# Block positions added to the tokens ahead of their split, and two more pieces ahead of the dilated groups' combination

## The chip, the cores and the metric

One core of a Trainium2 chip runs the whole kernel. The metric is device time in microseconds (us), from the start of one execution to its end. Engines are named as in the profile: PE is TensorE's matrix products, PEld its weight loads, DVE is VectorE, ACT is ScalarE, POOL is GpSimd, SP is SyncE, which issues the loads and stores.

## What is computed

One layer on 1024 tokens of width 1024. The input is projected by one wide matrix into the queries, keys and values of two mixers and their gates. Mixer A is attention in three dilated groups (dilation 1, 4, 16), whose outputs are weighted by a softmax over the groups' log-sums. Mixer B is sparse attention with three branches (compressed, selected, windowed). Both are merged by sigmoid gates, multiplied by an output matrix, normalised, and sent through a mixture of 32 experts, two for each token.

The change lies in two places: the combination of the dilated groups, and the compressed branch of mixer B. In the latter, blocks of 32 tokens with stride 16 (63 blocks, two key-value heads of width 64) get a learned position added to each token and go through a two-layer net:

```python
blocks = jnp.concatenate([chunks[:, r:r + n_cmp] for r in range(ratio)], axis=2)
blocks = blocks + pos_emb[:, None, :]
flat = blocks.transpose(0, 1, 3, 2, 4).reshape(B_, n_cmp, G, CMP_LEN * E)
return jax.nn.gelu(flat @ w1) @ w2
```

This is done twice, for keys ("k") and values ("v").

## The kernel before, in words

**Products in three passes.** Nearly every product of 32-bit data is made of three: both operands are split into a high part (a cast to the reduced 32-bit format, on ACT) and a low part (a subtraction, on DVE or POOL), and high x high, high x low and low x high are summed in PSUM. `split` (L120 to L125) does it for pages of 128x1024; its lines in the profile are L123 (ACT) and L124 (DVE or POOL).

**The stream and its pieces.** The projection is a list of 44 jobs, each one 128-column block of the input matrix (`jobs`, L519 to L533). `stream` (L222 to L242) runs a job as two halves of 512 tokens, each half as 8 steps over the contraction with three products (L233 to L235); every second step it yields. So a piece is six products, and a job is eight pieces. `chunk(n)` (L244) runs n pieces and counts them in `clock`. In the first piece of a job the next job's weights are split and the weights after that are loaded (`wsplit`, `wload`); there are two pages each for raw, high and low weights. When a half is complete, the job's sink takes it out of PSUM. The rest of the kernel up to the experts is written as a sequence of own products with `chunk` calls between them: the pieces fill TensorE's time while other engines work. The order of TensorE's instructions is exactly that of the program (L208). The other engines and SP are ordered by a planner from estimated times and the order of the program, and each then runs its queue in that order.

**The combination** (L554 to L614). The row statistics of the three dilated groups are turned by TensorE (12 groups of transposes, one piece behind each, L564 to L581), DVE and ACT make the group weights RW (L584 to L596), then `chunk(CCH)` with CCH = 6 runs at L597. Four rounds follow (L600 to L609): for each of three groups a product with a selector matrix (L605) spreads the weights over a bank (two banks, tag "pt"), DVE multiplies the group's output by it (L606), and POOL adds groups 1 and 2 onto group 0 (L609); one piece runs in each round, behind the second product. Each pair of rounds ends in a store (L610).

**The compression.** At L697 the pieces up to job 24 are run: `done` is 192, and the call runs `done - clock` of them, nine before. Then come the router's and gates' weights (loads L706 to L711, DVE and ACT L712 to L718, their product with ones L720, and products with the input, L739 and L740, with one piece behind each second step). During these pieces job 24, the tokens for k, is finished in two halves; job 26 brings those for v. Their sink is `cmp_sink` (L452 to L473): ACT copies the bank to a page "cr" (L455), then for each head, parity and half block ACT casts a strided view to CH (L469) and DVE subtracts to get CL (L470), eight of each per half. `compress` (L630 to L694) is a generator that is stepped between pieces: it loads the positions (L632), the second matrix (L635) and four pages of the first matrix (L639), splits these, and for each of 16 slices runs three products (L656 to L658). The positions do not pass through the tokens: DVE sums the slices of the first matrix, each row weighted by its position (L653, L655), into `acc`, and a product with a matrix of ones (L660) adds `acc` to each block's sum. Behind it come the activation (L663 to L669), transposes (L673), and the second matrix (L680, L688). The raw pages of the first matrix, "cr", and several others share four pages of tag "t".

Of the kernel before, what the change touches and what calls it, by code (L numbers as in the profile page):

```python
# [9 lines left out]
FP = mybir.dt.float32  # L10
# [4 lines left out]
OP = mybir.AluOpType  # L15
# [16 lines left out]
MG0 = 8  # L32
MG1 = 5
DLEAD = 3
CCH = 6
NLAG = 2
LEADW = 1
QEND = (15, 11)
# [39 lines left out]
def tile_hybrid(ctx: ExitStack, tc: tile.TileContext, x, xT, w_t, w_gate, pos_k, w1_k, w2_k, pos_v, w1_v, w2_v,  # L78
                w_a, w_b, w_out, w_oT, ln1_g, ln1_b, w_r, b_r, w_gu, w_dn, ln2_g, ln2_b, out, dbg=None):
    nc = tc.nc  # L80
# [78 lines left out]
    ones_f = k_pool.tile([128, 128], FP, name="ones_f")  # L159
# [15 lines left out]
    for k in range(8):  # L175
        r = s_pool.tile([128, 1024], FP, name=f"xr{k}")
        nc.sync.dma_start(r, xT[k * 128:(k + 1) * 128, :])
        raws.append(r)
        if k < 2:
            w = wraw("wr")  # L180
            nc.sync.dma_start(w, w_t[6 * k])
            first.append(w)
    for k in range(8):
        a, b = split(raws[k], xpage, xpage, "x")
# [264 lines left out]
            nc.sync.dma_start(mg[j, :, half * 512:half * 512 + 512], t)  # L449
        return sink  # L450

    def cmp_sink(CH, CL):  # L452
        def f(half, bnk):
            ps = tpage("cr", FP, (128, 512))
            nc.scalar.copy(ps, bnk)  # L455
            for g in range(2):
                v = ps[64 * g:64 * g + 64].rearrange("p (c l r) -> p r l c", l=8, r=2)
                for par in range(2):
                    b = slice(64 * par, 64 * par + 64)
                    for r in range(2):  # L460
                        c0, c1 = 32 * half, 32 * half + 32
                        if r == 0:
                            c1 = min(c1, 63)
                        else:
                            c0 = max(c0, 1)
                        src = v[:, par, :, c0 - 32 * half:c1 - 32 * half]
                        d = slice(63 * g + c0 - r, 63 * g + c1 - r)
                        hi = CH[b, 8 * r:8 * r + 8, d]
                        nc.scalar.activation(hi, src, AF.Copy)  # L469
                        nc.vector.tensor_tensor(CL[b, 8 * r:8 * r + 8, d], v[:, par, :, c0 - 32 * half:c1 - 32 * half],  # L470
                                                CH[64 * par:64 * par + 64, 8 * r:8 * r + 8, d].bitcast(FP),
                                                op=OP.subtract)
        return f  # L473

    C = {}
    N = []
    for G in range(2):
        sc = [[1.0 / (8.0 * BSLOPE[4 * G + 2 * p + i]) for i in range(2)] for p in range(2)]
# [25 lines left out]
    def c_sink(w):  # L504
        def sink(half, ps):
            if half == 0:
                C[w] = [t_pool.tile([128, 16, 126], FR, name=n, tag=n, bufs=1) for n in ("CH", "CL")]
            cmp_sink(*C[w])(half, ps)
        return sink

    def nsa_jobs(d):
# [16 lines left out]
    k, v, q = nsa_jobs(N[0])  # L528
# [98 lines left out]
    nc.vector.memset(kch.bitcast(FP), 0.0)  # L627
    nc.vector.memset(kcl.bitcast(FP), 0.0)

    def compress(pos, w1, w2, which):  # L630
        P = t_pool.tile([128, 16], FP, name="posT")
        nc.sync.dma_start(P, pos)  # L632
        W2 = t_pool.tile([128, 2, 2, 64], FP, name="w2")
        for i in range(2):
            nc.sync.dma_start(W2[:, :, i, :], w2)  # L635
        acc = t_pool.tile([128, 256], FP, name="sm", bufs=3)
        def prep(i):
            raw = tpage("w1")
            nc.sync.dma_start(raw.rearrange("p (l f) -> p l f", l=4), w1[:, 4 * i:4 * i + 4, :])  # L639
            return (raw,) + split(raw, thpage, tlpage, "w1")  # L640
        pre = [prep(0)]
        yield
        CH, CL = C[which]
        hp = bank("sc")
        for i in range(4):
            if i < 3:
                pre.append(prep(i + 1))
            raw, wh, wl = pre[i]
            for q in range(4):
                l = 4 * i + q  # L650
                f = slice(q * 256, q * 256 + 256)
                if l == 0:
                    nc.vector.tensor_scalar(acc, raw[:, f], P[:, 0:1], None, op0=OP.mult)  # L653
                else:
                    nc.vector.scalar_tensor_tensor(acc, raw[:, f], P[:, l:l + 1], acc, op0=OP.mult, op1=OP.add)  # L655
                nc.tensor.matmul(hp[:126, 0:256], CH[:, l, :], wh[:, f], start=l == 0, stop=False)  # L656
                nc.tensor.matmul(hp[:126, 0:256], CH[:, l, :], wl[:, f], start=False, stop=False)
                nc.tensor.matmul(hp[:126, 0:256], CL[:, l, :], wh[:, f], start=False, stop=False)  # L658
            yield
        nc.tensor.matmul(hp[:126, 0:256], ones_f[:, 0:126], acc, start=False, stop=True)  # L660
        u0 = t_pool.tile([128, 256], FP, name="sm", bufs=3)
        t = t_pool.tile([128, 256], FP, name="sm", bufs=3)
        nc.vector.tensor_copy(u0[:126], hp[:126, 0:256])  # L663
        nc.vector.tensor_tensor(t[:126], u0[:126], u0[:126], op=OP.mult)
        nc.vector.tensor_scalar(t[:126], t[:126], 0.044715, 1.0, op0=OP.mult, op1=OP.add)
        nc.vector.tensor_tensor(t[:126], t[:126], u0[:126], op=OP.mult)
        nc.scalar.activation(t[:126], t[:126], AF.Tanh, scale=math.sqrt(2.0 / math.pi))
        nc.vector.tensor_scalar(u0[:126], u0[:126], 0.5, None, op0=OP.mult)
        nc.vector.scalar_tensor_tensor(u0[:126], t[:126], 1.0, u0[:126], op0=OP.add, op1=OP.mult)  # L669
        yield  # L670
        pt = bank("pt")
        for ft in range(2):
            nc.tensor.transpose(pt[:, ft * 128:ft * 128 + 126], u0[:126, ft * 128:ft * 128 + 128], ident[:126, :126])  # L673
        u = t_pool.tile([128, 2, 2, 63], FP, name="sm", bufs=3)
        nc.scalar.copy(u.rearrange("p f g c -> p f (g c)"), pt[:, 0:256].rearrange("p (f m) -> p f m", f=2)[:, :, 0:126])
        yield
        ps = bank("av")
        if which == "k":
            for ft in range(2):
                nc.tensor.matmul(ps[:, :126], W2[:, ft].rearrange("p a e -> p (a e)"),  # L680
                                 u[:, ft].rearrange("p g c -> p (g c)"), start=ft == 0, stop=ft == 1)
            pv = ps[:, :126].rearrange("p (g c) -> p g c", g=2)
            nc.scalar.copy(kch[:, :, 0:63], pv)
            nc.vector.tensor_tensor(kcl[:, :, 0:63], pv, kch[:, :, 0:63].bitcast(FP), op=OP.subtract)
        else:
            for g in range(2):
                for ft in range(2):
                    nc.tensor.matmul(ps[0:63, g * 64:g * 64 + 64], u[:, ft, g, :], W2[:, ft, 0, :],  # L688
                                     start=ft == 0, stop=ft == 1)
            for g in range(2):  # L690
                nc.vector.memset(vcmp[g].bitcast(FP), 0.0)
                nc.scalar.copy(vcmp[g][0:63, 0:64], ps[0:63, g * 64:g * 64 + 64])
                nc.vector.tensor_tensor(vcmp[g][0:63, 64:128], ps[0:63, g * 64:g * 64 + 64],
                                        vcmp[g][0:63, 0:64].bitcast(FP), op=OP.subtract)  # L694

    done = 8 * (1 + 3 * 5 + MG0)
    chunk(done - clock[0])  # L697
    ck = compress(pos_k, w1_k, w2_k, "k")
    cv = compress(pos_v, w1_v, w2_v, "v")

    wr = tpage("wr", FP, (128, 8, 36))
    wb = t_pool.tile([128, 2, 36], FP, name="wb")
# [16 lines left out]
    ps = bank("sc")  # L719
# [1288 lines left out]
```

## Time and profile before

| what | value |
|---|---|
| median of 3 runs | 1700.71 us (1695.23 to 1700.79) |
| the profiled execution | 1701.19 us, span 1699.0 us |
| mean granted TensorE clock | 0.98 |
| PE busy | 1585.3 us (93% of the span) |
| DVE busy | 1252.2 us (74%) |
| ACT busy | 1114.8 us (66%) |
| POOL busy | 455.0 us (27%) |

The span reaches from the first to the last instruction. Busy times are summed over the whole span; where the engines stand in one stretch, a table by stretches tells. A wait is the idle time of an engine ahead of an instruction, put down to the instruction of another engine that ended last before it.

### The profile page before, as it was taken

What the parts mean: (1) busy time and instruction counts of PE and PEld (TensorE: products, weight loads), DVE (VectorE), ACT (ScalarE), POOL (GpSimd) and SP (SyncE); (2) the same over time, 40 slices, a digit from 0 to 9 for tenths busy, and PEclk for the clock granted to TensorE, in tenths of its full rate; (3) what the DMA queues carried; (4) which work ended last, traced back from release to release, by engine and by line L of the source; (5) the groups of instructions that cost most, each with busy time, mean ns of one, the idle gap of its engine ahead of it and who ended that gap; (6) DMA issues with size and microseconds to landing.
All of it is one profiled execution on the core that took longest, in us unless ns stands there. A gap on an engine that the chain in (4) does not pass through costs nothing. (4 is left out here: it accounts for less than half of the span.)

```text
span 1699.0 us, 24721 instructions
## 1 busy us (share of the span) xinstructions
PE 1585.3 (93%) x8109; PEld 1303.9 (77%) x8109; DVE 1252.2 (74%) x2740; ACT 1114.8 (66%) x2050; POOL 455.0 (27%) x416
## 2 busy tenths in 40 slices
PE   7999999998899999999789996999999999999991
PEld 6888888777778987788678995777777777777771
DVE  5555554247867774588877787889888998999994
ACT  4566665515557786477943112778898888889882
POOL 1011113341122333232620152133311231322242
PEclk9999999999999999999999997999999999999996
DMA  7111112232321010001363767999999999999982
GB/s 270 41 38 38 38 38 69 75 102 87 127 75 48 30 52 23 31 18 36 98 217 140 299 239 251 333 348 337 371 353 367 333 351 359 360 348 357 370 260 61
DMA packets 107362, 313.86 MB, mean 185 GB/s; under 512 B 22028, under 2 KB 26252, under 8 KB 107232
## 3 DMA queue, kind: packets, MB, share of 16 engines
q1 hardware_dynamic: 93936, 287.21, 46.4%
q0 software_dynamic: 13296, 25.05, 6.0%
q8 instruction: 65, 1.06, 0.3%
q14 instruction: 65, 0.53, 0.1%
HBM read 290.02 MB, written 46.98 MB: 198 GB/s over the span
## 5 line engine op out<-in xcount | busy, mean ns | idle before, releaser
L1507 DVE TENSOR_TENSOR el<-er,eh 128x1024 fp32r<-128x1024 f32 x384 | 448.6, 1219 | 36.3 <-ACT eh L1506 36.1
L1506 ACT CAST eh<-er 128x1024 fp32r<-128x1024 f32 x384 | 391.3, 1055 | 46.3 <-PE pt L1524 34.1
L233 PE MATMUL pp<-xh,wh 128*128 128x512 f32 x672 | 273.4, 407 | 1.6 <-DVE q L288 1.6
L235 PE MATMUL pp<-xh,wl 128*128 128x512 f32 x672 | 265.6, 395 | 0.0
L234 PE MATMUL pp<-xl,wh 128*128 128x512 f32 x672 | 264.2, 393 | 0.0
L1524 PE MATMUL av<-eh,xt 128*128 128x512 f32 x512 | 196.5, 394 | 1.5 <-ACT xt L1493 1.3
L1524 PE MATMUL pt<-eh,xt 128*128 128x512 f32 x512 | 197.2, 395 | 0.0
L235 PEld LDWEIGHTS pp<-xh,wl 128*128 128x128 f32 x672 | 127.1, 189 | 29.5
L233 PEld LDWEIGHTS pp<-xh,wh 128*128 128x128 f32 x672 | 127.4, 190 | 21.1 <-DVE q L288 2.0
L234 PEld LDWEIGHTS pp<-xl,wh 128*128 128x128 f32 x672 | 127.5, 190 | 19.5
L1524 PE MATMUL sc<-eh,at 128*128 128x512 f32 x512 | 142.1, 399 | 0.0
L898 POOL TENSOR_TENSOR pw<-pw,st 128x64 f32<-128x64 f32 (+5 forms) x128 | 86.0, 701 | 183.5 <-DVE st L893 154.3
L1550 POOL DMA_INDIRECT ybuf<-y,idx x30 | 84.8, 2827 | 173.6 <-ACT y L1549 166.3
L1524 PEld LDWEIGHTS av<-eh,xt 128*128 128x128 f32 x512 | 96.5, 189 | 24.9 <-ACT xt L1493 1.7
L1524 PEld LDWEIGHTS pt<-eh,xt 128*128 128x128 f32 x512 | 96.6, 189 | 22.7
L936 DVE TENSOR_TENSOR PT<-pt,PT 128x512 fp32r<-128x512 f32 (+1 forms) x136 | 91.0, 671 | 25.1 <-ACT PT L935 23.5
L1524 PEld LDWEIGHTS sc<-eh,at 128*128 128x128 f32 x512 | 93.3, 188 | 20.7 <-ACT eh L1506 0.8
L1524 PE MATMUL av<-el,xt 128*128 128x512 f32 x256 | 106.3, 415 | 3.0 <-DVE el L1507 2.2
L1524 PE MATMUL pt<-el,xt 128*128 128x512 f32 x256 | 101.0, 394 | 0.0
L124 POOL TENSOR_TENSOR wl<-wr,wh 128x1024 fp32r<-128x1024 f32 x24 | 59.0, 2459 | 137.4 <-ACT wh L123 118.0
L1401 POOL DMA_INDIRECT xg<-hbuf,idx x31 | 32.7, 1054 | 216.4 <-PE pp L1487 204.2
L935 ACT CAST PT<-pt 128x512 fp32r<-128x512 f32 (+1 forms) x136 | 76.8, 567 | 16.5 <-PE pt L928 14.9
(451 smaller groups left out, 3611.4 us busy)
## 6 DMA issues: line engine op xcount, KB each, us to landing
er<-in_w_gu_dram SPq DMA_DIRECT2D x256, 512.0 KB
er<-in_w_dn_dram SPq DMA_DIRECT2D x128, 512.0 KB
wr<-in_w_t_dram SPq DMA_DIRECT2D x44, 512.0 KB
mgd<-mg SPq DMA_DIRECT2D x32, 256.0 KB
G<-mgd SPq DMA_DIRECT2D x32, 256.0 KB
xr<-in_xT_dram SPq DMA_DIRECT2D x8, 512.0 KB
out_dram<-in_ln_b_dram SPq DMA_DIRECT2D x8, 512.0 KB
wo<-in_w_oT_dram SPq DMA_DIRECT2D x8, 512.0 KB
```

The source lines that it names most:

```text
L124: (eng or nc.vector).tensor_tensor(lo, raw, hi.bitcast(FP), op=OP.subtract)
L233: nc.tensor.matmul(ps, wh[:, kk], xh[k][:, c], start=k == 0, stop=False)
L234: nc.tensor.matmul(ps, wh[:, kk], xl[k][:, c], start=False, stop=False)
L235: nc.tensor.matmul(ps, wl[:, kk], xh[k][:, c], start=False, stop=k == 7)
L898: nc.gpsimd.tensor_tensor(t, t, st[:, 1, hi_, i:i + 1].to_broadcast([128, w]), op=OP.mult)
L935: nc.scalar.copy(t[:, 0], src)
L936: nc.vector.tensor_tensor(t[:, 1], src, t[:, 0].bitcast(FP), op=OP.subtract)
L1401: nc.gpsimd.indirect_dma_start(out=t, out_offset=None, in_=hbuf, in_offset=bass.IndirectOffsetOnAxis(ap=ids, axis=0), bounds_check=S - 1, ...
L1506: nc.scalar.copy(wh, r)
L1507: nc.vector.tensor_tensor(wl, r, wh.bitcast(FP), op=OP.subtract)
L1524: nc.tensor.matmul(pss[h], a[j == 1][:, kk], (wl if j == 2 else wh)[:, h], start=o == 0 and j == 0, stop=o == n - 1 and j == 2)
L1550: s_ = nc.gpsimd.indirect_dma_start(out=ybuf, out_offset=bass.IndirectOffsetOnAxis(ap=self.ids, axis=0), in_=y, in_offset=None, bounds_che ...
```

## The change

Positions are added to the tokens in the sink, in place of the weighted sum. The bank is read by DVE twice, once with the positions of the first 16 tokens of a block (r = 0) and once with those of the last 16 (r = 1), into one page of twice the width; the casts and subtractions read the one that belongs to their half block. `acc`, its 32 instructions for both tables and the product with ones go. The position table is now held as 32 values for each of the 64 channels, once for each head, and loaded in the first half of the sink by four loads (head x parity), in place of one load in `compress`; the table has one buffer. CCH goes from 6 to 8, so that `chunk(done - clock[0])` behind the combination runs two pieces fewer.

```diff
-CCH = 6
+CCH = 8
...
-    def cmp_sink(CH, CL):
+    def cmp_sink(CH, CL, pos):
         def f(half, bnk):
-            ps = tpage("cr", FP, (128, 512))
-            nc.scalar.copy(ps, bnk)
+
+            ps = tpage("cr", FP, (128, 2, 512))
+            for r in range(2):
+                nc.vector.tensor_tensor(ps[:, r].rearrange("p (c o) -> p c o", o=16), bnk.rearrange("p (c o) -> p c o", o=16),
+                                        pos[:, 16 * r:16 * r + 16][:, None, :].to_broadcast([128, 32, 16]), op=OP.add)
             for g in range(2):
-                v = ps[64 * g:64 * g + 64].rearrange("p (c l r) -> p r l c", l=8, r=2)
+                vs = [ps[64 * g:64 * g + 64, r].rearrange("p (c l r) -> p r l c", l=8, r=2) for r in range(2)]
...
-                        src = v[:, par, :, c0 - 32 * half:c1 - 32 * half]
+                        src = vs[r][:, par, :, c0 - 32 * half:c1 - 32 * half]
...
                 C[w] = [t_pool.tile([128, 16, 126], FR, name=n, tag=n, bufs=1) for n in ("CH", "CL")]
-            cmp_sink(*C[w])(half, ps)
+                P[w] = t_pool.tile([128, 32], FP, name="posT")
+                for g in range(2):
+                    o = P[w][64 * g:64 * g + 64].rearrange("p (l r) -> p l r", r=2)
+                    for par in range(2):
+                        nc.sync.dma_start(o[:, :, par], dict(k=pos_k, v=pos_v)[w][64 * par:64 * par + 64, :])
+            cmp_sink(*C[w], P[w])(half, ps)
...
-    def compress(pos, w1, w2, which):
-        P = t_pool.tile([128, 16], FP, name="posT")
-        nc.sync.dma_start(P, pos)
+    def compress(w1, w2, which):
...
-        acc = t_pool.tile([128, 256], FP, name="sm", bufs=3)
...
-                if l == 0:
-                    nc.vector.tensor_scalar(acc, raw[:, f], P[:, 0:1], None, op0=OP.mult)
-                else:
-                    nc.vector.scalar_tensor_tensor(acc, raw[:, f], P[:, l:l + 1], acc, op0=OP.mult, op1=OP.add)
...
-                nc.tensor.matmul(hp[:126, 0:256], CL[:, l, :], wh[:, f], start=False, stop=False)
+                nc.tensor.matmul(hp[:126, 0:256], CL[:, l, :], wh[:, f], start=False, stop=l == 15)
...
-        nc.tensor.matmul(hp[:126, 0:256], ones_f[:, 0:126], acc, start=False, stop=True)
```

## Rows read from the trace of the kernel before

**Rows 1.** Busy time by stretch: stretch, length, engines (instructions), PEclk, DMA share, GB/s

```profile
345.00:361.00 16.00, 12.72 (x40) 8.42 (x39) 10.90 (x17) 2.43 (x4) 8.08 (x8) 0.79 0.31 91
...
400.00:428.00 28.00, 22.17 (x113) 18.49 (x114) 22.96 (x38) 13.18 (x24) 5.37 (x6) 0.94 0.24 76
428.00:466.00 38.00, 33.18 (x170) 27.41 (x169) 34.30 (x54) 19.50 (x31) 7.13 (x4) 0.96 0.41 134
...
500.00:600.00 100.00, 99.86 (x640) 89.01 (x639) 75.84 (x251) 76.20 (x168) 36.35 (x36) 1.00 0.11 39
...
1200.00:1300.00 100.00, 98.16 (x443) 75.70 (x441) 88.55 (x109) 88.75 (x120) 23.12 (x14) 1.00 0.99 361
```

**Rows 2.** PE's waits, 300 to 500 us: us in total, times, longest

```profile
PE sc L660 <- DVE sm L655: 6.0, 2, 3.0
PE sc L657 <- DVE w1l L124: 2.9, 3, 1.9
PE pt L605 <- DVE rw L596: 1.9, 1, 1.9
PE sc L658 <- DVE CL L470: 1.6, 1, 1.6
```

**Rows 3.** Timeline of PE at the combination: start us, us, what, [idle before]

```profile
347.67 1.07 PE L605 MATMUL pt<-rw,sel 100*128 100x512 f32 x2 [1.87 <-DVE rw L596]
...
361.22 0.40 PE L233 MATMUL pp<-xh,wh 128*128 128x512 f32 x1
...
373.49 0.34 PE L720 MATMUL sc<-wb,ones_f 128*128 128x72 f32 x2
```

**Rows 4.** PE by the microsecond: stretch, length, busy, PEclk, DMA share, GB/s

```profile
349.00:350.00 1.00, 1.00 (x5) 0.73 0.00 0
...
356.00:357.00 1.00, 0.65 (x3) 0.86 0.00 0
```

**Rows 5.** Timeline of DVE behind the combination's products

```profile
358.50 1.98 DVE L606 TENSOR_TENSOR oT<-pt,oT 128x512 f32<-128x512 f32 x3 [0.93 <-PE pt L605]
...
369.61 0.69 DVE L715 TENSOR_TENSOR wgd<-wg,wgd 128x512 fp32r<-128x512 f32 x1 [3.91 <-ACT wgd L714]
```

**Rows 6.** Timeline of POOL at the combination's end

```profile
362.80 1.31 POOL L609 TENSOR_TENSOR oT<-oT,oT 128x512 f32<-128x512 f32 x1
...
364.93 2.43 POOL L124 TENSOR_TENSOR wl<-wr,wh 128x1024 fp32r<-128x1024 f32 x1
```

**Rows 7.** Timeline of SP's queue, same stretch: time of issue, queue time

```profile
358.65 0.74 SPq L708 DMA_DIRECT2D gbc<-in_ln_g_dram  x1
...
365.00 0.79 SPq L711 DMA_DIRECT2D wg<-in_w_gate_dram  x1
...
367.78 0.42 SPq L632 DMA_DIRECT2D posT<-in_pos_k_dram  x1
```

**Rows 8.** Timeline of PE at the end of the first compression

```profile
413.24 0.39 PE L233 MATMUL pp<-xh,wh 128*128 128x512 f32 x1
...
417.82 1.22 PE L660 MATMUL sc<-sm,ones_f 128*126 128x256 f32 x2 [3.03 <-DVE sm L655]
418.47 0.99 PE L233 MATMUL pp<-xh,wh 128*128 128x512 f32 x1
...
421.28 0.39 PE L233 MATMUL pp<-xh,wh 128*128 128x512 f32 x1
```

**Rows 9.** Two lines' instructions (ns min/median/max), and DVE's timeline at the activation chain's end

```profile
L655 DVE SCALAR_TENSOR_TENSOR sm<-w,posT,sm x30: 466/484/2703, 402.3 to 455.0; 128x256 f32<-128x256 f32 x30
...
L470 DVE TENSOR_TENSOR CL<-cr,CH x32: 567/586/1516, 385.0 to 440.2; 64x256 fp32r<-64x256 f32 x16, 64x248 fp32r<-64x248 f32 x16
...
422.24 0.42 DVE L669 SCALAR_TENSOR_TENSOR sm<-sm 126x256 f32<-126x256 f32 x1 [0.16 <-ACT sm L667]
```

**Rows 10.** Timeline of SP's queue ahead of the experts

```profile
932.82 8.94 SPq L1251 DMA_DIRECT2D z<-in_x_dram  x3
941.80 4.09 SPq L1559 DMA_DIRECT2D er<-in_w_gu_dram  x7
```

More of the change, by code (lines that the diff above doesn't have):

```diff
@@ L469, in f @@
                         nc.scalar.activation(hi, src, AF.Copy)
-                        nc.vector.tensor_tensor(CL[b, 8 * r:8 * r + 8, d], v[:, par, :, c0 - 32 * half:c1 - 32 * half],
+                        nc.vector.tensor_tensor(CL[b, 8 * r:8 * r + 8, d], src,
                                                 CH[64 * par:64 * par + 64, 8 * r:8 * r + 8, d].bitcast(FP),
@@ L473, in cmp_sink @@
         return f
-    C = {}
+    C, P = {}, {}
     N = []
@@ L697, in tile_hybrid @@
     chunk(done - clock[0])
-    ck = compress(pos_k, w1_k, w2_k, "k")
-    cv = compress(pos_v, w1_v, w2_v, "v")
+    ck = compress(w1_k, w2_k, "k")
+    cv = compress(w1_v, w2_v, "v")
     wr = tpage("wr", FP, (128, 8, 36))
```

## The prediction

> **What bounds the kernel now.** I read the stage table first [rows 1]. Between 500 and 600 us TensorE is busy 99.86 of 100 us: before the experts, the order of TensorE's work, written out by hand, is the clock of the kernel. From 1200 us on TensorE is busy 98.16 of 100 us at 361 GB/s; nothing in that part has a fixed date, its loads follow buffers that earlier work frees. So a microsecond that TensorE saves before 500 us should arrive at the end nearly whole. The three stretches that the diff touches stand out as holes: 345 to 361 us (12.72 of 16 busy, mean clock 0.79), 400 to 428 (22.17 of 28) and 428 to 466 (33.18 of 38). In the last two VectorE is busy 22.96 of 28 and 34.30 of 38 us: there it is the fullest engine. The list of TensorE's waits between 300 and 500 us names what ends the holes [rows 2]: 6.0 us in two waits of the ones product (L660) for the weight sums, 2.9 in three for the low part of a weight page (L657 on L124), 1.9 in one for the combination's first selector product (L605), 1.6 in one for the low part of the compressed tokens (L658). That is 12.4 us of bare waiting.
>
> The clock adds to it. Behind the 1.87 us wait before L605 [rows 3] the granted clock falls from 1.0 to half (1.2 GHz) between 349.5 and about 356.5 us [rows 4]. Behind the first L660 wait six ordinary products take 2.81 us, from 418.47 to 421.28 [rows 8], where full rate needs 6 x 0.227 = 1.36: 1.45 us lost.
>
> **Two more pieces (CCH).** A piece is six products; nine of them fill 361.22 to 373.49 us, 1.363 us each [rows 3]. Two more ahead of the combination are 2.73 us of work in front of L605, more than the 1.87 us wait. The weights RW it waits for do not depend on pieces, so the wait goes: **+1.87**. The combination itself runs 347.67 to 361.22, 13.55 us, half of it at half clock. At full clock its own work on TensorE is 12 products of 0.23 and four pieces of 1.36, 8.2 us; VectorE's 12 multiplies at 0.66 us [rows 5] are 7.9. With two banks, three products and a piece cannot repeat faster than piece, product, multiply, product: about 2.8 us, four times, 10.6 to 11 in all with the hand-overs. I take **+2.7**, ends 0 (the clock falls anyway) and 4.
>
> The two pieces are taken from behind the combination, where they are cover: seven are left of nine. What they cover is the gate and router weight: its low part (L715) ends at 369.61 + 0.69 = 370.30 us [rows 5], TensorE needs it right behind L720 at 373.49 [rows 3]. 3.2 us of slack less 2.73 leaves 0.5. Three things now lean on that slack. The weight job whose end frees a page now ends inside the combination (piece 184, third of its four, instead of first behind it), so the 2.43 us split on POOL (L124, at 364.93) can come ahead of POOL's last additions (one stood at 362.80) [rows 6], and the clearing of wg and its load (L711, 365.00) stand behind those. The freed page lets the next 512 KB weight load go earlier, beside wg's. And the position loads: below. Each could make wg 1 to 3 us late. Nearest is the POOL term, one split less the half that fits in gaps: I take a wait of **-1.5**, ends 0 and -5 (2.4 + 3.0 - 0.5). Sum of this part: 1.87 + 2.7 - 1.5 = **+3.1**.
>
> **Positions on the tokens.** Removed from VectorE: 30 multiply-adds at 0.484 us median [rows 9] and two first multiplies, for which I take no more than a multiply-add each: about 15 us. Removed from ACT: four copies of 128x512 (L455). Added to VectorE: eight additions of 128x512, one input in PSUM. Nearest is L606 at 0.66 (same shape, same memories): 5.3 us. The upper end is L470's rate, 0.586 for 256 strided columns, 1.17 each, 9.4 in all; I take 5.3, since both inputs run through 16 neighbouring elements before a jump. Either way VectorE is relieved, by 6 to 10 us. In the path through the sink ACT's copy of that shape becomes an addition of 0.66 ahead of ACT's first cast and a second that runs beside it; ACT in return has a copy less to do there. I count the sink as even.
>
> Then, on TensorE: both L660 waits go, **+6.0**; L660's own two passes take 417.82 to 418.47 = 0.65, twice [rows 8], **+1.3**; the half-clock stretch behind each, 1.45, twice, **+2.9** (the second taken like the first). The L657 waits come from VectorE doing sums ahead of a split: of 2.9 us I leave 1.2 (the splits still stand behind the token subtractions, and the second page of v behind its load), **+1.7**. The L658 wait arose as subtractions queued behind sums: of 1.6 I leave 0.3, **+1.3**. Next late is the activation chain (L663 to L669) that the transposes need: it now starts when the last L658 ends, and has a piece from 413.24 us plus three more, 5.4 us, for 3.6 us of its own (from 419.04, the end of L660, to 422.24 + 0.42 [rows 8, 9]) and three nk subtractions in the queue; **-0.5** for both halves, ends 0 and -5. Sum: 6.0 + 1.3 + 2.9 + 1.7 + 1.3 - 0.5 = **+12.7**.
>
> Nothing is charged for the shorter life of the raw weight pages (they are free after their split, no longer after the sums): it can only bring loads forward.
>
> **The position loads.** One load of 8 KB each (0.42 us of SP's queue at 367.78) becomes four of 4 KB whose elements land 8 bytes apart. The row nearest to that is the load of ln gains, 1024 elements of 4 bytes: 0.74 us of SP's queue [rows 7]. So some 3 us of SP per table instead of 0.4. For k they have from about 367 to 383 us, for v from the second k sink to the first v sink, some 30 us. I charge nothing beyond the term in the 1.5 above; ahead of L711 they would cost up to 3.0. The Trainium skill speaks against this load: "DMA: Bandwidth & Descriptors", section "Rules for kernel authors", says that a last dimension that is not contiguous becomes one descriptor per element. The trace agrees so far that the ln load held the queue longer than the contiguous one (0.74 against 0.42). By the page the term would stand at its lower end and the sum would be 3.5 us smaller.
>
> **Sum.** 3.1 + 12.7 = 15.8 us. The profiled execution took 1701.19 us (span 1699.0 and 2.2 around it), 0.5 above the median of 1700.71. 1701.19 - 15.8 = 1685.4, or 1684.9 from the median: I say 1685. A measurement here tells about 0.5%, 8.5 us, from no change.
>
> **Rivals.**
> 1. *The gate weight becomes the new wait.* POOL's split and the position loads both come ahead of wg: 5 us of wait at L739, and the clock falls behind it as it did behind 1.87 us (some 7 us at half, 3.4 lost). The first part turns from +3.1 to -3.8, and the total is 8.9: 1692. For it: only 0.5 us of slack is left. Against: wr, the ln gains and wg come earlier in the program than the position loads. Chance 0.17.
> 2. *The activation chain takes the place of the sums.* The mask work and nk subtractions that filled VectorE between sums stand ahead of L663; each half waits 2.5 us and drops the clock. -5 and -2.9: total 8.4, 1692. For it: VectorE is 90% busy at 428 to 466. Against: 15 us of that go away. Chance 0.15.
> 3. *Slower, by a new order of the loads at the experts' start.* All queues but TensorE's are ordered by a planner's own estimates, which shift from here on. At 932.82 three row loads (z) stand just ahead of a run of seven expert loads (941.80) on SP [rows 10]. If the plan puts expert loads ahead of z, the row stage that makes the routing starts later by 512 KB at 361 GB/s, 1.45 us for each. Eleven, 16 us, give all of the gain back; from there on it is slower, and seventeen, 24.7 us, end at 1710. For it: SP alone is planned there. Against: the row loads come first in the program. Chance 0.06.
> 4. *More than the sum:* no wait at wg and none at page starts, +1.5 + 1.5 + 0.5, and the combination at its upper end, +1.3: 1680. Chance 0.12.
> 5. *The sums go but their waits stay*, as the subtractions of the token sinks, now behind two additions, hold the splits: L660's terms (10.2) and 3.1 remain, less 1.5: total 11.8, 1689. Chance 0.12.
>
> My forecast, within 4 us of 1685, has the remaining 0.38. Faster by over 0.5% means below 1692.2: the forecast, 4 and 5, and half of 1 and 2, with the spread of the runs (1695.23 to 1700.79) about even: 0.75. Slower is rival 3: 0.06. The rest, 0.19, is the same. The range from 1677 to 1697 takes in all rivals but the third, and the ends of the unknown terms (0 to 4, 0 to -5, 0 to -5) as far as they don't fall together.
>
> **What would show it.** Right: no wait before L605 and clock 1.0 through the combination; L660 and L655 gone; the activation chain starting within 0.5 us of the last L658; L739 waiting under 2 us; the eight additions near 0.66 us. Wrong: a wait of over 3 us at L739 or L720, waits of over 2 us at L673, half clock in either stretch, additions over 1 us, or a hole of this size that opens behind 500 us.

## The result, and the profile after

The changed kernel takes 1687.2 us (median of five runs, 1685.11 to 1688.29) where the kernel before takes 1700.64 (1694.92 to 1700.79): a ratio of 0.9936 [0.9921, 0.9951], 13.4 us less. The profiled execution took 1687.2 us, its span is 1685.3 instead of 1699.0. I had said 1685.0 us, from 1677 to 1697.

The diff moves line numbers. In the kernel after, the combination's product is L613 (L605 before), its multiply L614, POOL's additions L617; the token subtractions are L473 (L470), the new additions L457; the three products of the compression are L657, L658 (the one with a page's low part) and L659 (L656 to L658). From L661 on the numbers are those of before.

Busy time by stretch, kernel after (columns as in [rows 1]):

```profile
345.00:361.00 16.00, 14.33 (x61) 10.81 (x60) 11.80 (x18) 3.88 (x6) 10.24 (x9) 1.00 0.28 102
...
400.00:428.00 28.00, 28.00 (x141) 23.93 (x140) 19.32 (x30) 17.28 (x28) 9.04 (x9) 0.94 0.22 48
428.00:466.00 38.00, 36.23 (x190) 29.43 (x189) 29.39 (x40) 19.68 (x30) 4.91 (x2) 1.00 0.55 181
500.00:600.00 100.00, 99.86 (x659) 89.53 (x658) 76.98 (x246) 76.53 (x174) 33.06 (x35) 1.00 0.12 40
```

The holes of [rows 1] are nearly filled: TensorE works 14.33, 28.00 and 36.23 us where it worked 12.72, 22.17 and 33.18, and the clock of the first stretch went from 0.79 to 1.00. VectorE is no longer the fullest engine from 400 to 428 us (19.32, was 22.96). One figure did not move, the 0.94 of the clock from 400 to 428, but its place did: the half clock stood behind the first wait at L660 and now stands behind the wait for k's first page.

TensorE's waits from 300 to 500 us, kernel after (us in total, times, longest):

```profile
PE sc L658 <- DVE w1l L124: 2.2, 2, 2.0
PE pt L613 <- DVE oT L614: 1.7, 3, 0.6
PE av L769 <- DVE wol L758: 1.5, 2, 0.8
PE sc L739 <- DVE wgd L715: 1.1, 1, 1.1
PE sc L659 <- DVE CL L473: 0.8, 1, 0.8
```

Of [rows 2], the wait for RW (1.9) and both waits for the sums (6.0) are gone. L739 on wgd is new, as forecast (1.12 us). A 2.0 us wait for a page's low part stays. Where they stand, in TensorE's timeline (start us, us, what, [idle before]):

```profile
348.56 0.62 PE L613 MATMUL pt<-rw,sel 100*128 100x512 f32 x2
...
359.13 0.40 PE L613 MATMUL pt<-rw,sel 100*128 100x512 f32 x1
...
369.30 0.44 PE L720 MATMUL sc<-wb,ones_f 128*128 128x72 f32 x2 [0.22 <-DVE wb L718]
370.86 0.50 PE L739 MATMUL sc<-xh,wgd 128*128 128x512 f32 x1 [1.12 <-DVE wgd L715]
...
399.35 0.38 PE L658 MATMUL sc<-w1l,CH 128*126 128x256 f32 x1 [2.03 <-DVE w1l L124]
...
431.73 0.39 PE L659 MATMUL sc<-w1h,CL 128*126 128x256 f32 x1 [0.83 <-DVE CL L473]
```

**How the gain builds up.** TensorE's order is fixed, so I compare kernels by marks: the start of one instruction on TensorE, counted from the last transposes of the row statistics (L569 before, L577 after; at 335.6 to 337.5 us in all kernels, and nothing ahead of them changes). Us behind that point, worked out from TensorE's timelines:

| mark | before | after | gained up to here |
|---|---|---|---|
| first selector product | 12.03 | 12.71 | (two more pieces, 2.73, ahead of it) |
| last selector product | 25.34 | 23.28 | |
| first product with the gate weight, L739 | 37.99 | 35.01 | 2.98 |
| first page of k | 64.49 | 61.14 | 3.35 |
| activation's transposes, k | 88.38 | 80.32 | 8.06 |
| first page of v | 102.73 | 94.65 | 8.08 |
| activation's transposes, v | 126.48 | 112.42 | 14.06 |
| first product of the sparse attention | 153.78 | 140.69 | 13.09 |

From that last mark to the end of the span it takes 1209.6 us before and 1208.8 after: in these two profiles what was gained ahead of 490 us arrives whole, as read from [rows 1]. But over all the kernels below, this same unedited stretch takes 1203.0 to 1210.8 us in single profiles, in no order that follows the edits. So parts are judged by marks, and only whole kernels by their ratios.

### The profile page after: what moved, and what is told of

Read it like the earlier page. It is cut to its first block, busy times and chain, and to the rows that moved or that the text cites. A ratio compares the mean times of both kernels' runs of the same rounds, so it can differ in the third digit from the quotient of the medians.

```text
span 1685.3 us, 24695 instructions
## 1 busy us (share of the span) xinstructions
PE 1583.9 (94%) x8105; PEld 1305.3 (77%) x8105; DVE 1241.6 (74%) x2716; ACT 1113.4 (66%) x2046; POOL 469.6 (28%) x416
## 3 DMA queue, kind: packets, MB, share of 16 engines
q8 instruction: 65, 1.06, 0.3%
## 5 line engine op out<-in xcount | busy, mean ns | idle before, releaser
L1550 POOL DMA_INDIRECT ybuf<-y,idx x30 | 103.3, 3444 | 172.0 <-ACT y L1549 151.0
L124 POOL TENSOR_TENSOR wl<-wr,wh 128x1024 fp32r<-128x1024 f32 x24 | 57.6, 2402 | 135.0 <-ACT wh L123 129.2
```

The lines of the kernel that those rows point to most:

```text
L124: (eng or nc.vector).tensor_tensor(lo, raw, hi.bitcast(FP), op=OP.subtract)
L1550: s_ = nc.gpsimd.indirect_dma_start(out=ybuf, out_offset=bass.IndirectOffsetOnAxis(ap=self.ids, axis=0), in_=y, in_offset=None, bounds_che ...
```

## The experiments

Two theories stood at the start. Mine: the two parts of the change act each in its own stretch, sizes as in the sum. The rivals: the wait at L739 comes from the position loads rather than from the moved pieces, and the page wait that stays is a matter of loads or clock rather than of VectorE's queue.

**Two more pieces alone (cch_only).**

```diff
-CCH = 6
+CCH = 8
```

> The kernel before with CCH = 8 and nothing else. Theory: the two edits add up, and this one is worth the 2.8 us by which the products with the input (L739) come earlier in the changed kernel: no wait before the first selector product, clock 1.0 through the combination, and a wait of 0.5 to 1.5 us at L720 or L739 remains, because the weight split on POOL now stands ahead of POOL's last additions and the router weights' loads wait behind those. Ratio to before about 0.998. Rival: the new wait at L739 comes from the four position loads on SP's queue; then it is gone here and the gain is 4.2 us. Second rival: the two pieces are worth nothing alone, since the cover they take from behind comes due in full; then L739 starts within 0.5 us of where it started before.

Measured: 0.9979 [0.9964, 0.9993]. L739 stands at 34.71 against 37.99, 3.28 us earlier, and 3.11 of it are still there at v's transposes (123.37 against 126.48). TensorE's timeline of this kernel:

```profile
370.94 0.44 PE L720 MATMUL sc<-wb,ones_f 128*128 128x72 f32 x2 [0.18 <-DVE wb L718]
372.23 0.50 PE L739 MATMUL sc<-xh,wgd 128*128 128x512 f32 x1 [0.84 <-DVE wgd L715]
```

No position load is changed here, yet 0.84 of the 1.12 us of wait is there: the moved pieces make it.

**Positions alone (pos_only)**: the kernel after with `CCH = 6`.

> The changed kernel with CCH = 6. Theory: the 1.87 us wait before the selector product and the half clock behind it are back, L720 and L739 wait for nothing, and the first transposes of the second activation (L673, v) come 11 us earlier than before; ratio to before 0.993 to 0.995 by its own gain of 10 to 11 us. The 2 us wait at the first page of k and the half clock behind it stay, since they depend on the sink and not on the pieces. Rival: the gain of the positions needs the pieces (the state of the clock or the planner's order differs), and the ratio is above 0.997.

Measured: 0.9943 [0.9925, 0.9961]. 1.88 us of wait for RW are back, none at L739 (37.15). At v's transposes it is 13.71 us ahead of before (112.77), where I had expected 11. The parts alone give 3.11 and 13.71, together 16.8; the change gives 14.06, 2.8 less. Of that, 1.1 is missing already at L739, mostly because the combination took 12.48 us here and 13.31 before, behind the same wait: its half clock was shorter in this profile. Another 1.4 is missing between the first page of k and k's transposes: 17.67 us here, 19.18 after (and 0.15 that cch_only loses there). Both kernels wait 2.0 us for the first page there, but only the kernel after has half clock behind it; I had expected it in both. TensorE's clock by the microsecond (stretch, length, busy, PEclk, DMA share, GB/s), after and then pos_only, both right behind that wait:

```profile
401.00:402.00 1.00, 1.00 (x4) 0.50 0.41 3
```

```profile
402.00:403.00 1.00, 1.00 (x10) 1.00 0.99 64
```

**Ten pieces (cch10)**: the kernel after with `CCH = 10`.

> The changed kernel with CCH = 10. Theory: cover is only moved; ahead of the selector product there is nothing left to hide, so 2.73 us more of waiting opens behind: L720 and L739 together wait 3.5 to 4.5 us instead of 1.34, the clock falls to half behind that wait, and the time is 3 to 5 us over the changed kernel (1690 to 1692). Rival: the router weights come earlier too, as pieces and weight splits move, and the time is within 1 us of the changed kernel.

Measured: 0.9958 [0.9944, 0.9972], 1689.3 us. The first selector product moves 2.72 us back and the wait at L739 grows from 1.12 to 4.07, 2.95 more; L739 itself ends up at 37.44, near where before had it (37.99).

```profile
373.26 0.72 PE L739 MATMUL sc<-xh,wgd 128*128 128x512 f32 x1 [4.07 <-DVE wgd L715]
```

The pieces stand ahead of L739 in either order, so a gate weight with a fixed date would leave L739 where it was. But its date moves along: its low part (L715) ends 34.96 us behind the last transposes after and 37.39 here, in both some 11.5 us behind the last selector product (11.68 and 11.42). VectorE's timeline, after and then this kernel:

```profile
370.12 0.69 DVE L715 TENSOR_TENSOR wgd<-wg,wgd 128x512 fp32r<-128x512 f32 x1 [0.87 <-ACT wgd L714]
```

```profile
372.51 0.69 DVE L715 TENSOR_TENSOR wgd<-wg,wgd 128x512 fp32r<-128x512 f32 x1 [4.32 <-ACT wgd L714]
```

So a piece too many ahead of the combination puts the weight off by nearly its own length, while TensorE wants it no later: it turns into wait, about one for one. This is the first rival of the prediction, with its price; some three microseconds of half clock stand behind this wait. The interval of the ratio still overlaps that of the change, so the loss is read from the marks.

**One position load for a table in place of four (pos_one_load)**: the host lays the table out as 128x32.

```diff
-                for g in range(2):
-                    o = P[w][64 * g:64 * g + 64].rearrange("p (l r) -> p l r", r=2)
-                    for par in range(2):
-                        nc.sync.dma_start(o[:, :, par], dict(k=pos_k, v=pos_v)[w][64 * par:64 * par + 64, :])
+                nc.sync.dma_start(P[w], dict(k=pos_k, v=pos_v)[w])
```

> The changed kernel with the position table laid out for it as 128 rows of 32 values, so that one contiguous load takes the place of the four with elements 8 bytes apart. Theory: the four loads cost nothing that TensorE sees, for they stand behind the gate weights' load on SP and the table is read 10 us later: the wait at L739 stays 1 to 1.5 us and the time stays within 0.5 us. Rival: their elements crowd the DMA engines while the gate weights land; then the wait at L739 falls below 0.5 us and the time by about 1 us.

Measured: 0.9918 [0.9887, 0.9949]; its interval overlaps that of the change, so the time tells nothing here. The wait at L739 is 0.82 against 1.12, between my theory (1 to 1.5) and its rival (below 0.5). The page's DMA line, after and then this kernel:

```profile
DMA packets 115395, 313.87 MB, mean 186 GB/s; under 512 B 30061, under 2 KB 34285, under 8 KB 115265
```

```profile
DMA packets 107362, 313.87 MB, mean 187 GB/s; under 512 B 22028, under 2 KB 26252, under 8 KB 107232
```

The eight loads are 8,033 packets below 512 B, about one for each of their 8,192 elements. In that the Trainium skill ("DMA: Bandwidth & Descriptors", section "Rules for kernel authors") holds: a last dimension that is not contiguous is one descriptor per element. Its price at L739 is 0.3 us, not the 3.5 that the lower end of my term gave.

**VectorE makes the low part of job 24's page (split24_dve).** It is POOL's 2.4 us split that falls into the combination.

```diff
-            wsp[i] = split(wsp[i], whi, wlo, "w", nc.gpsimd if i in POOLW else None)
+            wsp[i] = split(wsp[i], whi, wlo, "w", nc.gpsimd if i in POOLW and i != 24 else None)
```

> The changed kernel with one weight split (that of job 24, which falls into the combination) on VectorE in place of POOL. Theory: POOL's last additions end 2.4 us earlier, the store of ya, the gains' second load and the gate weights' load follow them on SP, and the waits at L720 and L739 (1.34 us in the changed kernel, 1.0 with one position load) go to 0; VectorE's 1.22 us in the combination costs less than 1 us there, so L739 comes 0.5 to 1.4 us earlier counted from the last transposes of the statistics (35.0 us in the changed kernel). Rival: the gate weights wait for bandwidth beside the 512 KB weight load issued just ahead of them, and the wait stays at 1 us or more.

Measured: 0.9929 [0.9902, 0.9957]. No wait is left at L720 or L739, and L739 stands at 33.23, 1.78 us earlier (I had expected 0.5 to 1.4); the combination ends at 23.30, as after, so the split costs VectorE nothing there. POOL's timeline in the kernel after, and then SP's queue after and in this kernel:

```profile
357.36 2.39 POOL L124 TENSOR_TENSOR wl<-wr,wh 128x1024 fp32r<-128x1024 f32 x1 [0.24 <-ACT wh L123]
...
363.16 1.30 POOL L617 TENSOR_TENSOR oT<-oT,oT 128x512 f32<-128x512 f32 x1
364.39 0.14 POOL L710 MEMSET wg<- 128x32 f32 x1
```

```profile
364.49 0.33 SPq L618 DMA_DIRECT2D yad<-oT  x1
364.88 0.43 SPq L708 DMA_DIRECT2D gbc<-in_ln_b_dram  x1
365.36 1.02 SPq L711 DMA_DIRECT2D wg<-in_w_gate_dram  x1
```

```profile
360.27 1.03 SPq L711 DMA_DIRECT2D wg<-in_w_gate_dram  x1
...
364.47 0.35 SPq L618 DMA_DIRECT2D yad<-oT  x1
```

Here is the path of the wait in the kernel after. The split comes ahead of POOL's last additions, which end at 364.46 (363.16 + 1.30); the store of the combined rows (L618) waits for them at the head of SP's queue; the gate weight's load is two places behind it. With the split off POOL the plan puts that load ahead of the store, 5.6 us earlier, counted from the last transposes (335.85 and 336.35). The last addition itself ends only 0.5 us earlier, since the plan now puts other POOL work ahead of it:

```profile
363.15 1.30 POOL L617 TENSOR_TENSOR oT<-oT,oT 128x512 f32<-128x512 f32 x1
```

So what this run removes is the gate load's place behind the store; the length of the split alone is not separated here.

**Seven pieces (cch7)**, a single run: the kernel after with `CCH = 7`.

> The changed kernel with CCH = 7. Theory: one piece covers 1.36 of the 1.87 us, a wait of 0.4 to 0.6 us is left ahead of the selector product, the clock stays at 1.0 through the combination, and of the waits at L720 and L739 nothing is left, since one more piece of cover stands behind: L739 at 35.0 to 35.6 us behind the last transposes of the statistics, as good as with 8 pieces. Rival: the split on POOL still stands ahead of the additions, and L739 waits 0.5 us or more all the same.

Measured: 1680.88 us, where before took 1701.13 on the same chip; one time alone gives no interval. L739 stands at 34.33, 0.68 us earlier than with eight pieces, and waits for nothing, though the selector product waits 0.51 us. POOL's split now stands behind all the additions: with a piece less, job 24's page is not yet due inside the combination.

```profile
362.22 2.64 POOL L124 TENSOR_TENSOR wl<-wr,wh 128x1024 fp32r<-128x1024 f32 x1
```

The gate weight's low part ends 8.45 us behind the last selector product, where after has 11.68 and before, whose split also stands behind, 9.32. So the place of that one split is worth 2.4 to 3.2 us of the weight's date. That the wait is gone does not need it: one more piece of cover (1.36 us) is as long as the waits of the kernel after (1.34). There is no half clock in this profile either, though the wait for k's first page is 2.08.

**The first page of k earlier (early_page).** The call that asks for the first page of the compression's weights moves from behind the router to ahead of the products with the gate weight.

```diff
+    next(ck)
     for half in range(2):
         c = slice(half * 512, half * 512 + 512)
...
     wo_ = router()
-    next(ck)
     chunk(3)
```

> The changed kernel with the first step of the k compression (its first page's load, cast and split) moved ahead of the products with the input. Theory: the 2.03 us wait at k's first page is the split queued on VectorE behind the token subtractions of the second sink half and two gate instructions; with the split done before, only the subtractions are left, which end 0.5 us after TensorE wants them. The wait falls to 0.3 to 0.9 us, no half clock follows, and the transposes of the k activation come 2.0 to 3.0 us earlier, at 77.3 to 78.3 us behind the last transposes of the statistics where the changed kernel has 80.3. Rival: the subtractions themselves end later (they share the stretch with POOL's weight split) and the wait stays over 1.5 us. Second rival: the page's load, ahead of the gate weights' work, makes L739 later by 1 us or more.

In the kernel after, VectorE's timeline shows why the page is late:

```profile
390.93 6.57 DVE L473 TENSOR_TENSOR CL<-cr,CH 64x248 fp32r<-64x248 f32 x8
397.53 0.26 DVE L746 TENSOR_SCALAR gates<-gates 128x192 f32<-128x192 f32 x1
397.71 0.45 DVE L747 TENSOR_SCALAR xW<-pt 128x288 f32<-128x288 f32 x1
398.07 2.35 DVE L124 TENSOR_TENSOR w1l<-w,w1h 128x1024 fp32r<-128x1024 f32 x2
```

The split (L124) is queued behind eight token subtractions and two gate instructions. Its cast stood in a queue too, behind ACT's eight token casts, and ends near 396.9 (395.83, two casts in 1.99):

```profile
395.83 1.99 ACT L123 CAST w1h<-w 128x1024 fp32r<-128x1024 f32 x2
```

So of the 2.03 us VectorE's queue holds the split for about 1.2 (396.9 to 398.07); the rest was already lost on ACT. Neither waited for the page's load. In early_page, VectorE's and TensorE's timelines:

```profile
374.32 1.23 DVE L124 TENSOR_TENSOR w1l<-w,w1h 128x1024 fp32r<-128x1024 f32 x1 [3.31 <-ACT w1h L123]
```

```profile
396.98 0.28 PE L657 MATMUL sc<-w1h,CH 128*126 128x256 f32 x1
397.10 0.28 PE L658 MATMUL sc<-w1l,CH 128*126 128x256 f32 x1
```

The split is done 22 us ahead of its use, L658 follows L657 without a wait and there is no half clock; 0.8 us of wait at a later page of k is left. k's transposes stand at 77.24 against 80.32, 3.08 us earlier. Measured: 0.9902 [0.9869, 0.9935], which overlaps the interval of the change. The edit asks for the load earlier as well, so it is the kernel after that rules out the rival (loads): there ACT took up the cast, without idling, as soon as it was through with the tokens, and the page's data were there.

**The same with six pieces (early_cch6).** What are the two pieces worth once that wait is gone?

> The changed kernel with the early first page and CCH = 6. It asks whether the two pieces are worth their own 2 to 3 us where the positions are on the tokens, since the profiles with CCH = 8 and 6 reached the v activation almost together (112.4 and 112.8 us behind the last transposes of the statistics): the one with 8 lost 1.5 us at half clock behind the first page's 2 us wait, the one with 6 did not. Theory: with that wait gone nothing is left to lose there, and CCH = 8 (109.4) is 1.5 to 3 us ahead at the v activation: 111 to 112.5 here. Rival: the pieces only move the wait, and the mark is within 0.7 us of 109.4.

Measured: 0.9918 [0.9892, 0.9943]. v's transposes stand at 112.87 (I had expected 111 to 112.5), with eight pieces (early_page) at 109.41: the pieces are worth 3.46 us there. Between pos_only and after they were worth 0.35 (112.77 against 112.42). Of the 3.1 between these, 1.5 is the half clock that after has behind the first page of k and pos_only has not, and 1.1 stands already at L739 (3.20 gained there by early_page, 2.14 by after), mostly since the combination took 13.28 us in early_cch6 and 12.48 in pos_only. So the pieces do not lose their worth beside the positions, and most of what seemed lost is where the clock happened to fall. The 3.46 has its share of that too: with a combination of 11.0 us, as sum_short below has it with six pieces and the same wait, I would estimate some 1.2.

**Both, and all three (both, three)**: early_page with split24_dve, then with the one load for each table as well.

> The two edits together. Theory: they touch different waits and add: L739 at 33.7 to 34.5 us behind the last transposes of the statistics, the k activation's transposes at 76 to 77.5, and the time 3 to 4 us under the changed kernel's (ratio to before 0.991 to 0.992). Rival: the clock falls somewhere else in the same stretch, and one of the two gains is given back.

> The changed kernel with the early first page, the combination's weight split on VectorE, and the position table in one contiguous load. Theory: the three add to a first attention product at 135.5 to 136.5 us behind the last transposes of the statistics (140.7 in the changed kernel, 153.8 before), 4 to 5 us earlier than the changed kernel, and the ratio to before is 0.989 to 0.991. Rival: the part from there to the end varies by more than that from plan to plan, and the ratio is no better than 0.9925.

Measured: 0.9893 [0.9858, 0.9928] and 0.9891 [0.9873, 0.9908]. L739 stands at 33.21 in each, k's transposes at 75.61 and 75.67, the first product of the sparse attention at 136.32 and 136.39, against 140.69 after: the two edits add up (3.38 and 1.06 alone, 4.37 here), and the single load brings nothing more. The interval of three lies wholly below that of the change, so there is a version that beats both kernels. That of early_page alone (0.9902) overlaps both, three's and the change's, so the time does not place it.

**Are the sums the backlog? (sum_short)** The kernel before, with 15 of the 16 multiply-adds of each position sum left out (the product with ones stays), a single run.

```diff
-                else:
-                    nc.vector.scalar_tensor_tensor(acc, raw[:, f], P[:, l:l + 1], acc, op0=OP.mult, op1=OP.add)
```

> The kernel before with 15 of the 16 steps of each weight sum left out (the positions of those slices are then missing), the ones product kept. It separates what VectorE's sums cost from what the product itself costs. Theory: the two waits ahead of L660 (3.03 and 2.97) and the half clock behind them are VectorE's backlog: they go to under 0.3 us, L660 keeps its 0.65 us each with its own hand-over, and the v activation's transposes come at 117 to 119 us behind the last transposes of the statistics (126.5 before, 112.8 with the positions on the tokens at CCH = 6). Rival: the backlog was the masks' and key subtractions' work, the waits shrink by half at most, and the mark stays above 121.

Measured: 1696.47 us, where before took 1695.97 on the same chip. (From L656 on its lines stand two lower than those of before.) Both waits for the sums are gone, so they were VectorE's backlog of sums. k's transposes stand at 81.94, 1.04 behind pos_only. Of what this kernel gains on before, 2.3 us are there at L739 already (35.68), ahead of any sum, by the clock in the combination. In v the time is not gained whole (119.76, between my theory's 117 to 119 and the rival's 121; pos_only 112.77, before 126.48). TensorE's timeline and then VectorE's:

```profile
456.19 0.41 PE L671 MATMUL pt<-ident,sm 126*128 126x126 f32 x2 [4.25 <-DVE sm L667]
```

```profile
448.34 0.42 DVE L662 TENSOR_TENSOR sm<-sm 126x256 f32<-126x256 f32 x1
451.88 1.22 DVE L756 TENSOR_TENSOR wol<-wo,woh 128x1024 fp32r<-128x1024 f32 x1 [3.13 <-ACT woh L755]
453.03 0.29 DVE L663 TENSOR_SCALAR sm<-sm 126x256 f32<-126x256 f32 x1
```

Between two steps of the activation chain (L662, L663) stands a split of the output weight that waits 3.13 us for its cast, so the transposes wait 4.25. This is the prediction's second rival, in another kernel: taking the sums away is not enough, the plan has to place what comes next well. In the kernel after it does:

```profile
448.27 0.38 PE L673 MATMUL pt<-ident,sm 126*128 126x126 f32 x2
```

## Why the prediction was right

**The two pieces.** Forecast +1.87 for the wait; it came to 2.05 (12.03 + 2.73 - 12.71). The combination: forecast +2.7, measured 2.74 (13.31 to 10.57 us from first to last selector product); the bound of 10.6 to 11 from the repeating piece, product, multiply, product was met. That the 2.7 came out so exactly is partly luck: it rests on half clock that other profiles, with the same wait, do not have (last section). The cover: forecast -1.5. From the last selector product to L739 it was 12.65 us, 9.92 without the two moved pieces, and it is 11.73: -1.81, of which 1.34 are waits at L720 and L739. The path was right, too: counted from the last selector product, the gate weight's low part ends 11.68 us behind it, before 9.32. That is 2.36 later, the whole length of POOL's split, of which I had let a part fit into gaps; less the slack of 0.6 it makes 1.8. Sum 2.98 against +3.1. Of the three causes I named for the cover, the split on POOL is the main one (its delay fits the 2.36, and split24_dve takes the wait away, by the order of SP's queue), the position loads are worth 0.3, and that a freed page lets a load go earlier was not tried.

**The positions.** Both waits at L660, its products and the half clock behind them: forecast 6.0 + 1.3 + 2.9 = 10.2, and by the trace of before and what is absent after, 6.0 + 1.3 + 2.9 again. The waits for the low part of the tokens went from 1.62 to 0.83, +0.8 where I had +1.3. The activation chain costs 0, not -0.5: the transposes wait for nothing. The additions took 0.680 us at the median (forecast 0.66):

```profile
L457 DVE TENSOR_TENSOR cr<-pp,posT x8: 678/680/690, 380.4 to 425.4; 128x512 f32<-128x512 f32 x8
```

and the sink is even, as counted: from the end of the half's last product to its last token subtraction 8.0 us before and after (second half of k).

**The term that failed** is that of L657 (now L658), "+1.7: the splits still stand behind the token subtractions". I named the right obstacle and took it for the smaller part. At k's first page the sums held that split up very little (0.34 us by VectorE's timeline of before); the subtractions on VectorE and the casts on ACT held it, and they stay. k's first page waits 2.03 (1.91 before), its later one 0 (0.77), v's 0.16 (0.24): +0.7 in waits. Behind the first one the clock is at half for three microseconds, which takes back about 1.1 (4.71 us gained from k's first page to its transposes, where the terms above make 5.78). In all about -0.3 instead of +1.7. That clock is what I had listed as a sign of being wrong, and it cost 1 us rather than the case.

**The end of the sum.** 15.8 forecast, 14.06 at v's transposes; 1 us goes behind them, where a second wait of 0.77 for the output weight's low part (L769) has joined one of 0.76; 13.1 at the sparse attention, 13.7 in the span, 13.4 in the medians.

**The rivals.** 1 is real but not here: a wait of 1.12 at L739, and 4.07 only at ten pieces. 2 does not happen in the changed kernel, and does in sum_short. 3: no sign, the stretch behind 490 us is 0.8 us shorter, well inside its scatter. 4 is about where early_page, both and three lie (1680.15, 1680.22 and 1681.84 us), by edits the change does not make. 5 was wrong for the sums and in part right for k's first page, which waits 2 us: 1.2 of it behind the subtractions, the rest behind ACT's casts of the same tokens.

## What to carry to other kernels

Where one engine's order is fixed and the others' queues are in order, price an edit by what stands in the queue ahead of the late instruction, entry by entry: removing the loudest neighbour (the sums) frees only the waits that it alone made, and the split behind the subtractions stayed late until it was asked for earlier. Work moved ahead as filler is worth its time while it fills a wait. Past that it only puts off what comes behind it: where the next late item (here the gate weight) hangs on that, each piece turns into wait, and a queue entry that slips ahead (POOL's split) counts as much as a piece or two. Measure parts from a common instruction on the fixed engine when a later stretch scatters by more than the parts are worth.

## What the hardware showed that I had not expected

How the clock answers a short wait is not fixed by the length of the wait. The wait of about 2 us for k's first page is followed by half clock (1.2 GHz) in the kernel after, cch10, pos_one_load, split24_dve and sum_short (1.91 to 2.04 us), and by full clock in before, pos_only, cch_only and cch7 (1.91 to 2.08). The wait of 1.87 to 1.88 us ahead of the combination is followed by about 7 us of half clock in before and in early_cch6, by a shorter stretch in pos_only, and by none in sum_short. Behind longer waits it fell every time: the four for the sums (2.97 to 3.03 us, before and cch_only), 4.07 in cch10 and 4.25 in sum_short. Two of these, early_cch6 and then sum_short, TensorE's clock (columns as above):

```profile
348.00:352.00 4.00, 3.52 (x11) 0.74 0.01 2
352.00:356.00 4.00, 4.00 (x9) 0.50 0.17 66
```

```profile
348.00:352.00 4.00, 2.88 (x11) 1.00 0.13 52
```

In sum_short the combination, with six pieces and the same wait ahead, took 11.00 us from first to last selector product, in before 13.31. So most of the +2.7 that I counted for it was the clock of one profiled execution, and in another it might have been 0.4. The Trainium skill ("TensorE: Matmul & The Clock Gate", section "What's actually happening") calls how many products run at the slow clock at a kernel's start "run-variable"; these rows, in mid-kernel, show the like. What decides it in one execution stays open; a term of the sum that rests on half clock behind a wait of 2 us should carry an end at nothing.
